# A hybrid attention and Fourier block: the Fourier input projection on sums and differences of mirrored tokens and weight columns, woven into the gate and z products, with y held in DRAM

## The chip, the cores and the metric

The kernel runs on one core of a Trainium2 chip. The metric is the time of one execution on the device in microseconds (us). Three runs of the kernel before took 2622.81 to 2623.37 us, with a median of 2623.29.

## The reference

One layer over 256 tokens of 4096 channels. After an RMS norm one wide projection gives q, k, v, the gating paths z of both branches, the Fourier input u and the gates. Attention and a two-dimensional Fourier transform work side by side; each is gated by silu(z), projected, weighted with a sigmoid gate, summed, projected again and added to x.

```python
h = rms_norm(x, norm_gain[layer])
proj = h @ w_in[layer]                       # 4096 -> 22528 columns
q, k, v, z_attn, u_four, z_four, gates = jnp.split(proj, offsets, axis=-1)
...                                          # 24 heads of 128, three dilations, softmax over all keys
branch_attn = (o_attn * jax.nn.silu(z_attn)) @ w_branch_attn[layer]

u = u_four.reshape(b, s, FOURIER_GROUPS, FOURIER_GROUP_DIM)       # 8 groups of 256 channels
y_four = jnp.fft.fft2(u, axes=(1, 3), norm="ortho").real.reshape(b, s, FOURIER_WIDTH)
branch_four = (y_four * jax.nn.silu(z_four)) @ w_branch_fourier[layer]

g_attn, g_four = jnp.split(gates + gate_bias[layer], N_BRANCHES, axis=-1)
mixed = jax.nn.sigmoid(g_attn) * branch_attn + jax.nn.sigmoid(g_four) * branch_four
x = x + mixed @ w_out[layer]
return rms_norm(x, final_norm_gain)
```

## The kernel before

Everything large is a product of an activation with 512 columns of a weight matrix. `gemm` (line 202) makes one: both token tiles (two of 128 tokens: the even and the odd ones) times 512 columns, in fp32r with three passes, since activation and weight are each split into a high and a low part: `wh` with `h_hi`, `wl` with `h_hi`, `wh` with `h_lo`. Such a product over 4096 channels has 16 steps of two slices of 128 channels, and a step has 2 x 2 x 3 = 12 matmuls of 512 columns. A 1 MB tile `wt` (four slices, 512 columns, fp32) is loaded by SyncE's queue (SP) for every second step. For each step ACT copies two slices of it to `wh` and VectorE (DVE) subtracts that from `wt` and writes `wl` (`split`, line 143). `wt`, `wh` and `wl` have three buffers each; `turn` (line 197) hands them out by turns.

The order of the products is: 2 for z of the attention (ZA), 9 for q, k, v of half the heads, 4 gates, 9 for the other half, 4 gates, the first z of the Fourier branch (ZF), then U and ZF by turns with 5 gates among them, 3 last gates; then the branches (eight pairs over 8 and 16 slices) and eight products with `w_out`. U is the Fourier input: 4 products. Each fills an accumulator pair, `u_of` copies it (with the norm's factor), `over_tokens` and `over_channels` transform it with short fp32 matmuls over the constant `dft_t` and with additions on VectorE, multiply with silu(z), transpose in 32x32 blocks and split into `y_hi` and `y_lo`, the left operand of the Fourier branch.

All that is not a product is a task: a generator that yields, before each stage, its time on VectorE and how many steps it must wait. `step` (line 126) runs once per step of a product and lets tasks go on as far as a credit allows, `BUDGET` per step. `finish` (line 119) runs tasks to their end at once. Every engine keeps the order in which the program writes its instructions (`InOrder`), so a task's stage lies in each engine's queue where `step` or `finish` put it, and an instruction that waits holds all that stands behind it on its engine. That holds for DMAs on SP too. The queue of loads runs ahead of the work only as far as the three `wt` buffers let it.

```python
def load(k):
    ...
    if k % WG == 0:
        wt = turn("wt", [P, WG, CW], F32)
        ...
            sp.dma_start(wt[:, q:q + n, :], wv[:, k + q:k + q + n, :])
    wh = turn("wh", [P, WS, CW], F32R)
    wl = turn("wl", [P, WS, CW], F32R)
    split(wt[:, k % WG:k % WG + WS, :], wh, wl)
```

The heads of the attention (`attend`) are tasks as well: scores on TensorE, mask and maximum on VectorE, the exponential on ACT, sixteen 32-row transposes on VectorE, then the product with v.

Of the kernel before, what the change touches and what calls it, by code (L numbers as in the profile page):

```python
# [17 lines left out]
P = 128  # L18
# [13 lines left out]
FW = SEQ // 4 + 1  # L32
# [3 lines left out]
GA = 4  # L36
GF = (), (8,), (9,), (10, 11, 12)
BUDGET = 1.35
CAP = 1.5
# [6 lines left out]
class InOrder:  # L46
    """An engine whose instructions keep the order that they are written in."""
# [9 lines left out]
class Clock:  # L57
    now = 0
    credit = 0.0


class Task:
# [15 lines left out]
def hybrid_block(ctx: ExitStack, tc: tile.TileContext, x, norm_gain, w_in, gate_bias, w_attn,  # L78
# [20 lines left out]
    # the function table, while the first loads are under way  # L99
# [3 lines left out]
    gates_d = dram.tile([NT, P, 2 * D], F32, name="gates_d")  # L103

# [1 line left out]
    # A task is a generator that yields, before each of its stages, the stage's time on VectorE in  # L106
    # us and the least number of steps since the stage before.
# [11 lines left out]
    def finish(these):  # L119
        while any(t in tasks for t in these):  # L120
            for t in list(these):
                finish(t.after)
                if t in tasks and not t.run(clock.now):
                    tasks.remove(t)

    def step():
        clock.now += 1
        clock.credit = min(clock.credit + BUDGET, CAP)
# [128 lines left out]
    def use(task):  # L257
        """The task that reads the product just made."""
        users[turns["acc"] % 2] = [spawn(task)]
        return users[turns["acc"] % 2]  # L260

# [1 line left out]
    h_hi = lhs.tile([P, KT, SEQ], F32R, tag="l_hi", name="h_hi")  # L263
    h_lo = lhs.tile([P, KT, SEQ], F32R, tag="l_lo", name="h_lo")
    szp = ctx.enter_context(tc.tile_pool(name="szp", bufs=1))
    sz = szp.tile([P, NT, 2 * CW], F32, tag="sz", name="sz")
# [49 lines left out]
    def norms():  # L316
        for i in range(NX):
            yield BUDGET, 0
# [8 lines left out]
    def silu(dst, ps, r):  # L327
        """dst = z * sigmoid(z), z = ps * r"""
# [4 lines left out]

    def silu_za(c, accs):
        if c == 0:
            yield from norms()
        for t in range(NT):
            yield from silu(sz[:, t, c * CW:(c + 1) * CW], accs[t], rstd[t])

    def gates(tiles, chunks):  # L340
        def gate(c, accs):
            bias, _ = tiles()
            nc.gpsimd.dma_start(bias, gate_bias[0:1, c * CW:(c + 1) * CW].to_broadcast([P, CW]))
            for t in range(NT):
                _, sg = tiles()
                yield 0.75, 0
                dve.scalar_tensor_tensor(sg, accs[t], rstd[t], bias, op0=ALU.mult, op1=ALU.add)
                yield 0.0, 1
                act.activation(sg, sg, AF.Sigmoid)
                nc.gpsimd.dma_start(gates_d[t, :, c * CW:(c + 1) * CW], sg)  # L350

        for c in chunks:
            accs = new_accs()
            gemm(accs, h_hi, h_lo, w_in, G0 + c * CW)
            use(gate(c, accs))

# [1 line left out]
    for c in range(2):  # L358
        accs = new_accs()
        gemm(accs, h_hi, h_lo, w_in, ZA0 + c * CW, **(dict(during=x_ahead, loading=x_loads) if c == 0 else {}))  # L360
        use(silu_za(c, accs))
    xs.close()

# [1 line left out]
    with ExitStack() as st:  # L365
        gp = pool(st, "gp", bufs=2)
        ap = pool(st, "ap")
        at = pool(st, "at", bufs=2)
        qp = pool(st, "qp", bufs=9)
# [60 lines left out]
        def gate_tiles():  # L430
            return gp.tile([P, CW], F32, name="bias"), gp.tile([P, CW], F32, name="sg")

        for half in range(2):
            got, made = {}, []
            for g in range(NG):
                for name, c0, fill, shape in (("q", Q0, rotated, [P, HC, SEQ]), ("k", K0, rotated, [P, HC, SEQ]),
                                              ("v", V0, values, [P, NT, CW])):
                    accs = new_accs()
                    gemm(accs, h_hi, h_lo, w_in, c0 + g * 1024 + half * CW)
                    got[name, g] = qp.tile(shape, F32, tag="qkv", name=name)  # L440
# [18 lines left out]
    with ExitStack() as st:  # L459
        fp = pool(st, "fp")  # L460
        ft = pool(st, "ft", bufs=2)
# [9 lines left out]
        flat = spawn(attn_transposed(), False)  # L471
        dft_t = fp.tile([P, NT, 2 * FW], F32, name="dft_t")
        nc.gpsimd.dma_start(dft_t, dft.rearrange("t p k -> p t k"))
        H = SEQ // 4

        def zf_of(accs, zf):
            for t in range(NT):
                yield from silu(zf[:, t, :], accs[t], rstd[t])

        def u_of(accs, u):  # L480
            # u's even and odd channels of each group, side by side
            for t in range(NT):
# [4 lines left out]
        def over_tokens(u, ab, d, ps):
            # cosine and sine sums over the tokens, from those over the even and the odd ones
            yield 0.0, 1
            pt = ps.tile([P, CW], F32, name="pt" if ps is ps_t else "sc")  # L490
            for t in range(NT):
                pe.matmul(pt[:, 2 * FW * t:2 * FW * (t + 1)], u[:, t, d, :], dft_t[:, t, :], start=True, stop=True)
            yield 0.0, LEAD
            eo = ft.tile([P, 2, 2, FW], F32, name="eo")
            act.activation(eo.rearrange("p t s k -> p (t s k)"), pt[:, :4 * FW], AF.Copy)

            def part(t, s, back):
                k = eo[:, t, s, H:0:-1] if back else eo[:, t, s, 0:H]
                return k.rearrange("p (m q) -> p m q", q=2)

            def place(s, i):
                o = ab[:, d, s, :].rearrange("p (q m) -> p m q", q=2)
                return o[:, i * H // 2:(i + 1) * H // 2, :]

            yield 1.1, 1
            for s in range(2):
                dve.tensor_add(place(s, 0), part(0, s, False), part(1, s, False))
                dve.tensor_sub(place(s, 2), part(0, s, False), part(1, s, False))
                dve.tensor_sub(place(s, 1), part(s, s, True), part(1 - s, s, True))
            dve.tensor_add(place(0, 3), part(0, 0, True), part(1, 0, True))  # L510
            dve.scalar_tensor_tensor(place(1, 3), part(0, 1, True), -1.0, part(1, 1, True),
                                     op0=ALU.mult, op1=ALU.subtract)

        def over_channels(zf, ab, c, gi, t, ps):
            yield 0.0, 1
            pt = ps.tile([P, CW], F32, name="pt" if ps is ps_t else "sc")
            for q in range(2):
                for s in range(2):
                    k = (q * 2 + s) * FW
                    pe.matmul(pt[:, k:k + FW], ab[:, gi * 2 + q, s, t * P:(t + 1) * P],  # L520
                              dft_t[:, q, s * FW:(s + 1) * FW], start=True, stop=True)
            yield 0.0, LEAD
            eo = ft.tile([P, 2, 2, FW], F32, name="eo")
            act.activation(eo.rearrange("p t s k -> p (t s k)"), pt[:, :4 * FW], AF.Copy)
            yield 1.3, 1
            lo = ft.tile([P, 2, FW], F32, name="lo")
            dve.tensor_add(lo, eo[:, 0], eo[:, 1])
            hi = ft.tile([P, 2, FW], F32, name="hi")
            dve.tensor_sub(hi, eo[:, 0], eo[:, 1])
            y = ft.tile([P, SEQ], F32, name="y")  # L530
            dve.tensor_sub(y[:, 0:H], lo[:, 0, 0:H], lo[:, 1, 0:H])
            dve.tensor_add(y[:, 2 * H - 1:H - 1:-1], hi[:, 0, 1:FW], hi[:, 1, 1:FW])
# [204 lines left out]
```

## Time and profile before

| | us |
|---|---|
| median of three runs | 2623.29 |
| span of the profiled execution | 2621.5 |
| TensorE (PE) busy | 2599.3 (99%) |
| VectorE (DVE) busy | 1724.1 (66%) |
| ACT busy | 1119.6 (43%) |
| GpSimd (POOL) busy | 41.1 (2%) |
| moved by DMA | 525.09 MB, 200 GB/s on average |

The profiled execution's own time is its span, 2621.5 us, which lies 1.8 us below the median of the runs. PE matmuls overlap in the pipeline, so a matmul's cost is read from the distance between starts and not from its length. A plain fp32 matmul (the short ones on `dft_t`, `q`, `pT`) leaves two records, an fp32r one leaves one. SPq and POOLq are the queues on which SyncE and GpSimd issue DMAs. All helpers have one line in the profile (L54), so groups are told apart by the names of their tiles.

### The profile page before, as it was taken

The page shows a single profiled execution, that of the slowest core. Times are in us where ns is not written, and L with a number is a line of the kernel's source. Part 1 is how long each engine was busy: PE and PEld are TensorE (multiplying, and loading weights), DVE is VectorE, ACT ScalarE, POOL GpSimd, SP SyncE. Part 2 cuts the span into 40 slices and gives each one's busy share as a digit, 9 for nine tenths or more (in the row PEclk, how much of TensorE's full clock was granted, in tenths as well). Part 3 has the DMA queues.
Part 4 walks back from the last instruction along what each step waited for, and adds up shares of the span by engine and source line. Part 5 has one row for each costly group of instructions (what it writes and reads, how often), then busy time and mean ns, then how long its engine had stood idle before and what let it go on. Part 6 is the DMA issues. An engine that isn't in the chain of part 4 may idle for free.

```text
span 2621.5 us, 29991 instructions
## 1 busy us (share of the span) xinstructions
PE 2599.3 (99%) x11617; PEld 2147.9 (82%) x11617; DVE 1724.1 (66%) x2847; ACT 1119.6 (43%) x1220; POOL 41.1 (2%) x74
## 2 busy tenths in 40 slices
PE   8999999999999999999999999999999999999998
PEld 7888888888888888888888888888888777888886
DVE  5566666776675757667587675757445888845554
ACT  5534343445434343444444444444444333444443
POOL 0000000000000000000000000000000000000000
PEclk9999999999999999999999999999999999999999
DMA  7655555556655555565655655556766666666674
GB/s 251 214 194 195 194 193 193 188 194 201 192 194 195 195 194 195 181 195 195 198 188 190 205 177 188 194 178 211 242 213 201 212 215 215 212 198 217 213 248 147
DMA packets 257936, 525.09 MB, mean 200 GB/s; under 512 B 9232, under 2 KB 9504, under 8 KB 257792
## 3 DMA queue, kind: packets, MB, share of 16 engines
q1 hardware_dynamic: 251344, 501.25, 58.3%
q0 software_dynamic: 6448, 21.91, 2.6%
q8 instruction: 91, 1.49, 0.2%
q14 instruction: 53, 0.43, 0.0%
HBM read 510.54 MB, written 12.58 MB: 200 GB/s over the span
## 4 chain that ended last, share of the span: by engine, by line
PE 99%; DVE 0%; DMA 0%; ACT 0%; SPq 0%; issue 0%; DVEq 0%; ACTq 0%
PE acc L54 97%; PE pt L54 1%; PE sc L54 1%; DVE wl L54 0%; DMA xt<-in_x_dram 0%; ACT u L54 0%; SPq L54 0%; DVE res L54 0%; ACT junk L54 0%; DVEq L733 0%; DVE nt L54 0%; ACT std L54 0%; DVE r L54 0%; DVE ssq L54 0%; DVE rstd_o L54 0%
## 5 line engine op out<-in xcount | busy, mean ns | idle before, releaser
L54 DVE TENSOR_TENSOR wl<-wt,wh 128x1024 fp32r<-128x1024 f32 x928 | 1134.9, 1225 | 823.0 <-ACT wh L54 817.5
L54 ACT ACTIVATE wh<-wt 128x1024 fp32r<-128x1024 f32 x928 | 980.4, 1059 | 1356.9 <-PE acc L54 1266.9
L54 PE MATMUL acc<-wh,h_hi 128*128 128x512 f32 x2816 | 1102.1, 391 | 0.0
L54 PE MATMUL acc<-wh,h_lo 128*128 128x512 f32 x2816 | 1096.9, 390 | 0.0
L54 PE MATMUL acc<-wl,h_hi 128*128 128x512 f32 x2816 | 1096.4, 389 | 0.0
L54 PEld LDWEIGHTS acc<-wh,h_lo 128*128 128x128 f32 x2816 | 528.9, 188 | 110.5
L54 PEld LDWEIGHTS acc<-wl,h_hi 128*128 128x128 f32 x2816 | 529.4, 188 | 108.3
L54 PEld LDWEIGHTS acc<-wh,h_hi 128*128 128x128 f32 x2816 | 529.3, 188 | 107.7
L54 PE MATMUL acc<-wl,m_hi 128*128 128x512 f32 x512 | 199.6, 390 | 0.0
L54 PE MATMUL acc<-wh,m_hi 128*128 128x512 f32 x512 | 199.6, 390 | 0.0
L54 PE MATMUL acc<-wh,m_lo 128*128 128x512 f32 x512 | 199.6, 390 | 0.0
L54 PEld LDWEIGHTS acc<-wh,m_lo 128*128 128x128 f32 x512 | 96.1, 188 | 20.7
L54 PEld LDWEIGHTS acc<-wh,m_hi 128*128 128x128 f32 x512 | 96.1, 188 | 20.6
L54 PEld LDWEIGHTS acc<-wl,m_hi 128*128 128x128 f32 x512 | 96.1, 188 | 20.3
L54 PE MATMUL acc<-wl,y_hi 128*128 128x512 f32 x256 | 101.1, 395 | 0.0
L54 PE MATMUL acc<-wh,y_lo 128*128 128x512 f32 x256 | 101.1, 395 | 0.0
L54 PE MATMUL acc<-wh,y_hi 128*128 128x512 f32 x256 | 101.0, 395 | 0.0
L54 DVE STREAM_TRANSPOSE mT<-m 32x128 f32<-32x128 f32 x256 | 77.4, 302 | 3.8
L54 DVE STREAM_TRANSPOSE pT<-pe 32x128 f32<-32x128 f32 x256 | 77.2, 302 | 4.0
L54 DVE STREAM_TRANSPOSE yT<-y 32x64 f32<-32x64 f32 x256 | 60.3, 236 | 3.6
L54 DVE STREAM_TRANSPOSE q<-m 32x128 f32<-32x128 f32 x192 | 58.0, 302 | 3.1
L54 DVE STREAM_TRANSPOSE k<-m 32x128 f32<-32x128 f32 x192 | 58.0, 302 | 3.1
(104 smaller groups left out, 1003.1 us busy)
## 6 DMA issues: line engine op xcount, KB each, us to landing
wt<-in_w_in_dram SPq DMA_DIRECT2D x351, 1024.0 KB, 5.1
wt<-in_w_out_dram SPq DMA_DIRECT2D x64, 1024.0 KB, 5.5
wt<-in_w_branch_fourier_dram SPq DMA_DIRECT2D x32, 1024.0 KB, 5.5
wt<-in_w_branch_attn_dram SPq DMA_DIRECT2D x16, 1024.0 KB, 5.5
ga<-gates_d POOLq DMA_DIRECT2D x16, 512.0 KB, 7.0
xt<-in_x_dram SPq DMA_DIRECT2D x16, 256.0 KB, 7.4
gates_d<-sg POOLq DMA_DIRECT2D x16, 256.0 KB, 2.7
gates_d<-z POOLq DMA_DIRECT2D x16, 256.0 KB, 3.8
```

The source lines that it names most:

```text
L54: return lambda *a, **k: self.tc.keep_in_program_order(f(*a, **k))
```

## The change

**The Fourier input.** The transform over 256 tokens and 256 channels has mirror symmetry: cosine sums need only x[s] + x[256-s], sine sums only x[s] - x[256-s], along both axes. The change makes these sums and differences before the product. `fold` makes them of the tokens of h (with the norm's factor from `norm_rows`): 128 folded rows of sums and 128 of differences, split into `f_hi` and `f_lo`; token 128 stands apart (`h128`). `u_sums` makes them of the weight's columns, in place in the raw tile `wu` (sums, 2 x 129 = 258 columns for two groups) and in `wo` (differences, 2 x 127 = 254), and gathers token 128's part on VectorE (`ea`). `u_split` splits them with ACT and VectorE; `u_multiply` multiplies: sums with sums and differences with differences, 2 slices x 2 x 3 = 12 matmuls of 258 or 254 columns. The 4 U products of 768 matmuls of 512 columns go.

**Where it stands.** These 64 u steps (two halves of the channels, four blocks of 512 columns, eight pairs of slices) lie between the steps of 12 products, nine gates and the four ZF: `u_hook` runs at each step of them, one u step every three steps, its three parts by turns.

```diff
+    def u_load(n):
...
+            raws[n] = U["fp"].tile([P, 2, CW], F32, name=f"wu{n % 2}")
...
+            sp.dma_start(raws[n], w_in[k * P:(k + 2) * P, c0:c0 + CW].rearrange("(k p) n -> p k n", p=P))
...
+        for j in range(2):
+            dve.tensor_tensor(o[:, j], near[:, j], far[:, j], op=ALU.subtract)
+            dve.tensor_tensor(near[:, j], near[:, j], far[:, j], op=ALU.add)
...
+                dve.scalar_tensor_tensor(a, e, row, a, op0=ALU.mult, op1=ALU.add)
...
+    def u_split(n):
+        w, o = raws.pop(n).rearrange("p k (g i) -> p k g i", g=2), parts[n]
+        uh, ul = (turn(v, [P, WS, CW], F32R) for v in ("wh", "wl"))
+        for src, s in ((w[:, :, :, 0:FW], slice(0, 2 * FW)), (o, slice(2 * FW, CW))):
+            for j in range(2):
+                h, l = (a[:, j, s].rearrange("p (g i) -> p g i", g=2) for a in (uh, ul))
+                act.activation(h, src[:, j], AF.Copy)
+                dve.tensor_tensor(l, src[:, j], h.bitcast(F32), op=ALU.subtract)
...
+                pe.matmul(out_, a, uh[:, j, s], start=(k == 0), stop=False)
+                pe.matmul(out_, a, ul[:, j, s], start=False, stop=False)
+                pe.matmul(out_, b, uh[:, j, s], start=False, stop=(k == HK - 1))
...
+        n, i = h // 3, h % 3
+        if i == 0:
+            if 0 < n <= len(usteps):
+                u_multiply(n - 1)
+            if n < len(usteps):
+                u_sums(n)
+        elif n < len(usteps):
+            if i == 1:
+                u_split(n)
+            else:
+                u_load(n + 2)
...
+    gates(1, at=(8, x_done))
+    u_load(0)
+    u_load(1)
+    clock.budget = BUDGET_U
+    for kind in "ggggggzgzzgz":
```

`wu` has two buffers. In the stretch `wh` and `wl` have a fourth buffer (`spare_u`). The budget of other tasks there is 0.9 instead of 1.35.

**The transform.** `mix` is a task per block of 512 columns. For each of two groups it has five fp32 matmuls of 130 columns (over tokens), eight ACT copies that put cosine and sine parts in order, four fp32 matmuls of 256 columns (over channels) and one multiplication with silu(z). The result y is written to `y_d` in DRAM. The tasks `over_tokens` and `over_channels` with their butterflies go.

```diff
+            y = U["ft"].tile([P, NT, SEQ], F32, name="y")
+            dve.tensor_tensor(y, ys.rearrange("p (t n) -> p t n", t=NT), zfs[c][:, :, g * SEQ:(g + 1) * SEQ], op=ALU.mult)
+            n0 = c * CW + g * SEQ
+            nc.gpsimd.dma_start(y_d[:, :, n0:n0 + SEQ].rearrange("t p n -> p t n"), y)
```

**The order of the products.** Gate 0 (during which x is transposed, as ZA was), gate 1 (norms, then `folding`), the stretch of 12, the two ZA, then the attention with one gate behind half 0 and three behind half 1 (`GA`), two gates during which y is read back (`yb`), transposed on TensorE and split (`y_transposed`), then branches and output as before. The heads of half 0 may run on into half 1 and are finished at its fourth product; q, k and v have 12 buffers instead of 9. `finish` now runs each task to its end before the next.

```diff
-        while any(t in tasks for t in these):
-            for t in list(these):
-                finish(t.after)
-                if t in tasks and not t.run(clock.now):
+        for t in list(these):
+            finish(t.after)
+            while t in tasks:
+                if not t.run(clock.now):
                     tasks.remove(t)
...
+                    if len(got) == 3:
+                        finish(heads)
...
+            gates(GA[half])
+        finish(heads)
```

**The order on SP.** Before, in any product: each load waits for the DMA semaphore that it reuses (DMAHW) and for VectorE (DVE), which frees its buffer. Behind `wt` stands the buffer's number.

```order
L54 DMA wt2_1127<-in_w_in_dram 128x4x512 [waits DMAHW5_49,DVE_49]
L54 DMA wt0_1178<-in_w_in_dram 128x4x512 [waits DMAHW6_49,DVE_49]
L54 DMA wt1_1203<-in_w_in_dram 128x4x512 [waits DMAHW7_49,DVE_49]
L54 DMA wt2_1243<-in_w_in_dram 128x4x512 [waits DMAHW0_49,DVE_49]
L54 DMA wt0_1282<-in_w_in_dram 128x4x512 [waits DMAHW1_49,DVE_49]
```

In the stretch of the changed kernel, `wu0` and `wu1` are the raw weights of the u steps:

```order
L55 DMA wt2_2034<-in_w_in_dram 128x4x512 [waits DMAHW5_49]
L55 DMA wu0_2066<-in_w_in_dram 128x2x512 [waits DMAHW6_49,DVE_49]
L55 DMA wt0_2080<-in_w_in_dram 128x4x512 [waits DMAHW7_49]
L55 DMA wt1_2143<-in_w_in_dram 128x4x512 [waits DMAHW0_49]
L55 DMA wu1_2149<-in_w_in_dram 128x2x512 [waits DMAHW1_49,DVE_49]
L55 DMA wt2_2198<-in_w_in_dram 128x4x512 [waits DMAHW2_49]
L55 DMA wu0_2230<-in_w_in_dram 128x2x512 [waits DMAHW3_49,DVE_49]
L55 DMA wt0_2244<-in_w_in_dram 128x4x512 [waits DMAHW4_49]
L55 DMA wu1_2307<-in_w_in_dram 128x2x512 [waits DMAHW6_49,DVE_49]
```

The wait for VectorE moved from every `wt` to the `wu` loads, and the `wt` loads stand behind these in the queue.

**The order on VectorE at the same place.** Before, in a product of the attention: the two `wl` of each `wt`, two steps to a tile.

```order
L54 TENSOR_TENSOR wl2_2011<-wt1_2008,wh2_2010 128x1024 [waits DMAHW7_49,Activation_49]
L54 TENSOR_TENSOR wl0_2027<-wt1_2008,wh0_2026 128x1024 [waits Activation_49]
L54 TENSOR_TENSOR wl1_2045<-wt2_2042,wh1_2044 128x1024 [waits DMAHW0_49,Activation_49]
L54 TENSOR_TENSOR wl2_2061<-wt2_2042,wh2_2060 128x1024 [waits Activation_49]
L54 TENSOR_TENSOR wl0_2096<-wt0_2093,wh0_2095 128x1024 [waits DMAHW1_49,Activation_49]
```

In the stretch, a u step's sums (`wo`, `wu1`, `ea0`) stand before the second `wl` of `wt0`, its splits (`wl3` from `wu1`, then from `wo`) behind it, and the next `wt1` after these:

```order
L55 TENSOR_TENSOR wl0_1555<-wt2_1526,wh0_1554 128x1024 [waits Activation_49]
L55 TENSOR_TENSOR wl1_1575<-wt0_1572,wh1_1574 128x1024 [waits DMAHW5_49,Activation_49]
L55 TENSOR_TENSOR wo_1590<-wu1_1461 128x254 [waits DMAHW2_49,DVE_49]
L55 TENSOR_TENSOR wu1_1461<-wu1_1461 128x2x127 [waits DVE_49]
L55 TENSOR_TENSOR wo_1590<-wu1_1461 128x254
L55 TENSOR_TENSOR wu1_1461<-wu1_1461 128x2x127 [waits DVE_49]
L55 SCALAR_TENSOR_TENSOR ea0_774<-wu1_1461,h128_772,ea0_774 128x258
L55 SCALAR_TENSOR_TENSOR ea0_774<-wu1_1461,h128_772,ea0_774 128x258 [waits DVE_49]
L55 TENSOR_TENSOR wl2_1610<-wt0_1572,wh2_1609 128x1024 [waits Activation_49]
L55 TENSOR_TENSOR wl3_1614<-wu1_1461,wh3_1613 128x258 [waits Activation_49] x2
L55 TENSOR_TENSOR wl3_1614<-wo_1590,wh3_1613 128x254 [waits Activation_49] x2
L55 TENSOR_TENSOR wl0_1638<-wt1_1635,wh0_1637 128x1024 [waits DMAHW6_49,Activation_49]
```

The `wu1` here is the buffer that a later `wu1` load on SP overwrites; its last readers on VectorE are the two `wl3` from `wu1`.

**The order on VectorE at the end of the attention.** Before, where the last head ends (`pT` its transposes, `sz` its result), with gate and ZF products running on:

```order
L54 TENSOR_TENSOR wl2_9223<-wt1_9220,wh2_9222 128x1024 [waits DMAHW0_49,Activation_49]
L54 STREAM_TRANSPOSE pT_9182<-pe_9144 32x4x32 x4
L54 TENSOR_TENSOR wl0_9243<-wt1_9220,wh0_9242 128x1024 [waits Activation_49]
L54 STREAM_TRANSPOSE pT_9182<-pe_9144 32x4x32 x4
L54 TENSOR_TENSOR wl1_9289<-wt2_9286,wh1_9288 128x1024 [waits DMAHW1_49,Activation_49]
L54 TENSOR_TENSOR wl2_9293<-wt2_9286,wh2_9292 128x1024 [waits Activation_49]
L54 SCALAR_TENSOR_TENSOR sg_9283<-acc10_8925,rstd_x_130,bias_9279 128x512 [waits DMASW7_49,DMASW5_49,PE_49]
L54 TENSOR_TENSOR wl0_9312<-wt0_9309,wh0_9311 128x1024 [waits DMAHW2_49,Activation_49]
L54 SCALAR_TENSOR_TENSOR sg_9318<-acc11_8926,rstd_x_130,bias_9279 128x512 [waits DMASW0_49,PE_49]
L54 TENSOR_TENSOR wl1_9333<-wt0_9309,wh1_9332 128x1024 [waits DVE_49,Activation_49]
L54 SCALAR_TENSOR_TENSOR sz_92<-pt_9262,rden_9180,sz_92 128x128
L54 TENSOR_TENSOR wl2_9354<-wt1_9351,wh2_9353 128x1024 [waits DMAHW3_49,DVE_49,Activation_49]
```

In the changed kernel, from the maximum of the last head but one to the first `wl` of the next product:

```order
L55 TENSOR_REDUCE mx_14366<-sm_14364 128x1 [waits DVE_49]
L55 TENSOR_SCALAR nm_14368<-mx_14366 128x1 [waits DVE_49]
L55 RECIPROCAL rden_14373<-den_14370 128x1 [waits Activation_49]
L55 STREAM_TRANSPOSE pT_14375<-pe_14371 32x4x32 x16
L55 SCALAR_TENSOR_TENSOR sz_6913<-pt_14392,rden_14373,sz_6913 128x128 [waits DVE_49,PE_49]
L55 TENSOR_TENSOR sm_14402<-sc_14398,mask_t_7203 128x512 [waits PE_49]
L55 TENSOR_REDUCE mx_14404<-sm_14402 128x1 [waits DVE_49]
L55 TENSOR_SCALAR nm_14406<-mx_14404 128x1 [waits DVE_49]
L55 RECIPROCAL rden_14411<-den_14408 128x1 [waits Activation_49]
L55 STREAM_TRANSPOSE pT_14413<-pe_14409 32x4x32 x16
L55 SCALAR_TENSOR_TENSOR sz_6913<-pt_14430,rden_14411,sz_6913 128x128 [waits DVE_49,PE_49]
L55 TENSOR_TENSOR wl0_14457<-wt1_14454,wh0_14456 128x1024 [waits DMAHW1_49,Activation_49]
```

Between the two last heads and behind them stood `wl` of running products; now none does until the last `sz`.

More of the change, by code (lines that the diff above doesn't have):

```diff
@@ L31 @@
 SCALE = DH ** -0.5
[L32 removed]
+FW = P + 1
+UK = 16
 WG = 4
@@ new lines, in hybrid_block, with gates, folding @@
+    gated = [0]
+    def gates(n, after=(), **kw):
+        for _ in range(n):
+            c = gated[0]
+            gated[0] += 1
+            accs = new_accs()
+            gemm(accs, h_hi, h_lo, w_in, G0 + c * CW, **kw)
+            use(gate(c, accs), after)
+    fo = ctx.enter_context(ExitStack())
+    U = {}
+    HK = KT // 2
+    def folding():
+        fp = U["fp"] = pool(fo, "fp")
+        U["ft"] = pool(fo, "ft")
+        spare.append(pool(fo, "spare_u"))
+        dft_t = fp.tile([P, 906], F32, name="dft_t")
+        nc.gpsimd.dma_start(dft_t, dft)
+        U["ct"], U["st"], U["at"] = (dft_t[:, 130 * i:130 * (i + 1)] for i in range(3))
+        U["cc"], U["sc"] = dft_t[:, 390:390 + SEQ], dft_t[:, 390 + SEQ:390 + 2 * SEQ]
+        U["sgn"] = dft_t[:, 902:903]
+        U["hi"] = fp.tile([P, HK, 2, P], F32R, name="f_hi")
+        U["lo"] = fp.tile([P, HK, 2, P], F32R, name="f_lo")
+        U["h128"] = fp.tile([P, KT], F32, name="h128")
+        U["rows"] = fp.tile([P, SEQ], F32, name="rows")
+        U["ea"] = [fp.tile([P, 2, 2, FW], F32, name=f"ea{c}") for c in range(4)]
+        U["od"] = [fp.tile([P, 2, P], F32, name=f"od{c}") for c in range(4)]
+        U["z"] = fp.tile([P, 2, P], F32, name="z")
+        for a in [U["z"], *U["od"]]:
+            nc.gpsimd.memset(a, 0.0)
+        U["norm"] = spawn(norm_rows(), False)
+        U["fold"] = [U["norm"]]
+        for b in range(HK // 4):
+            U["fold"].append(spawn(fold(b), False, U["fold"][-1:]))
@@ new lines, in norm_rows @@
+    def norm_rows():
+        ones = U["ft"].tile([P, P], F32, name="ones")
+        nc.gpsimd.memset(ones, 1.0)
+        dg = U["ft"].tile([P, NT, P], F32, name="dg")
+        yield 0.0, 0
+        for t in range(NT):
+            act.activation(dg[:, t, :], ident, AF.Copy, scale=rstd[t])
+        yield 0.0, 1
+        sc = ps_s.tile([P, CW], F32, name="sc")
+        for t in range(NT):
+            pe.matmul(sc[:, t * P:(t + 1) * P], ones, dg[:, t, :], start=True, stop=True)
+        yield 0.0, 1
+        act.activation(U["rows"], sc[:, :SEQ], AF.Copy)
@@ new lines, in u_hook, with zf_of @@
+    def u_hook(k):
+        if k < 0:
+            return
+        h = hooks[0]
+        hooks[0] += 1
+        n, i = h // 3, h % 3
+        if i == 0:
+            if 0 < n <= len(usteps):
+                u_multiply(n - 1)
+            if n < len(usteps):
+                u_sums(n)
+        elif n < len(usteps):
+            if i == 1:
+                u_split(n)
+            else:
+                u_load(n + 2)
+    zfs, zf_made = {}, {}
+    def zf_of(c, accs):
+        zf = zfs[c] = U["ft"].tile([P, NT, CW], F32, name="zf")
+        for t in range(NT):
+            yield from silu(zf[:, t, :], accs[t], rstd[t])
@@ new lines, in hybrid_block, with x_done @@
+    accs = new_accs()
+    gated[0] = 1
+    gemm(accs, h_hi, h_lo, w_in, G0, during=x_ahead, loading=x_loads)
+    normed = spawn(norms())
+    use(gate(0, accs), [normed])
+    def x_done():
+        finish([normed])
+        xs.close()
+        folding()
+    gates(1, at=(8, x_done))
[3 more added lines that the diff above has]
+    for kind in "ggggggzgzzgz":
+        if kind == "g":
+            gates(1, during=u_hook)
+        else:
+            c = len(zf_made)
+            accs = new_accs()
+            gemm(accs, h_hi, h_lo, w_in, ZF0 + c * CW, during=u_hook)
+            finish(mixing)
+            zf_made[c] = use(zf_of(c, accs))
@@ L334, in silu_za, with mixed @@
+    clock.budget = BUDGET
     def silu_za(c, accs):
-        if c == 0:
-            yield from norms()
         for t in range(NT):
             yield from silu(sz[:, t, c * CW:(c + 1) * CW], accs[t], rstd[t])
[L340 to L355, printed above, removed]
+    def mixed():
+        finish(mixing)
+        spare.clear()
+        fo.close()
@@ L487, in over_tokens @@
[L487 to L532, printed above, removed]
-            dve.tensor_sub(y[:, 2 * H:3 * H], hi[:, 0, 0:H], hi[:, 1, 0:H])
-            dve.tensor_add(y[:, 4 * H - 1:3 * H - 1:-1], lo[:, 0, 1:FW], lo[:, 1, 1:FW])
-            dve.tensor_mul(y, y, zf[:, t, gi * SEQ:(gi + 1) * SEQ])
-            yT = ft.tile([P, 2, P], F32, name="yT")
-            yield from flipped(yT, blocks(y))
-            b = c * 4 + gi * 2
-            yield from splitting(yT, y_hi[:, b:b + 2, t * P:(t + 1) * P], y_lo[:, b:b + 2, t * P:(t + 1) * P])
```

218 lines of the change are left out of this document (140 added, 78 removed).

## The prediction

> **What bounds the kernel now.** I read the page's busy line first, then the chain that ended last, the idle time of the costliest groups, the waits, and last a stretch of the timeline.
>
> ```profile
> span 2621.5 us, 29991 instructions
> PE 2599.3 (99%) x11617; PEld 2147.9 (82%) x11617; DVE 1724.1 (66%) x2847; ACT 1119.6 (43%) x1220; POOL 41.1 (2%) x74
> PE 99%; DVE 0%; DMA 0%; ACT 0%; SPq 0%; issue 0%; DVEq 0%; ACTq 0%
> ```
>
> TensorE is busy for 99% of the span and makes up 99% of the chain: nothing else ends last anywhere but at the edges. Its timeline shows what one product costs:
>
> ```profile
> 899.64 0.39 PE L54 MATMUL acc<-wh,h_hi 128*128 128x512 f32 x1
> 899.87 0.39 PE L54 MATMUL acc<-wl,h_hi 128*128 128x512 f32 x1
> 900.09 0.39 PE L54 MATMUL acc<-wh,h_lo 128*128 128x512 f32 x1
> 900.32 0.39 PE L54 MATMUL acc<-wh,h_hi 128*128 128x512 f32 x1
> ```
>
> Three starts take 0.68 us, so a 512-column matmul is worth 0.2267 us whatever its recorded length. A step of 12 takes 2.72, a product of 16 steps 43.5. The engines that feed it have slack, and where that slack lies is the point of this forecast:
>
> ```profile
> L54 DVE TENSOR_TENSOR wl<-wt,wh 128x1024 fp32r<-128x1024 f32 x928 | 1134.9, 1225 | 823.0 <-ACT wh L54 817.5
> L54 ACT ACTIVATE wh<-wt 128x1024 fp32r<-128x1024 f32 x928 | 980.4, 1059 | 1356.9 <-PE acc L54 1266.9
> SPq L54 <- DVE wl L54: 2198.2, 431, 12.0
> 579.88 18.62 SPq L54 DMA_DIRECT2D wt<-in_w_in_dram  x4
> wt<-in_w_in_dram SPq DMA_DIRECT2D x2, 1024.0 KB, 5.0
> 10.00:20.00 10.00, 9.93 (x39) 8.15 (x40) 6.17 (x9) 5.57 (x9) 0.00 (x0) 1.00 1.05 392
> ```
>
> ACT waits for TensorE to free a `wh`; VectorE waits for ACT; SyncE's queue waits for VectorE to free a `wt`, and issues at once when it does. Four 1 MB issues lie in 18.62 us, one per 5.44. A transfer lands 5.0 us after its issue (DMA view from 579.85 to 585.3 us), but it was issued two to three buffers (11 to 16 us) ahead of its use. So 5 us of latency is hidden by lead alone. The last row (a window of the start, where DMA is full) gives 392 GB/s as the rate when transfers queue up.
>
> **What the change removes.** Four U products: 768 x 0.2267 = 174.1 us. The old Fourier matmuls:
>
> ```profile
> L54 PE MATMUL sc<-dft_t,ab 128*128 128x65 f32 x64 | 8.5, 275 | 0.0
> L54 PE MATMUL pt<-dft_t,u 128*128 128x130 f32 x32 | 6.0, 294 | 0.9 <-ACT u L54 0.6
> 682.48 1.06 PE L54 MATMUL pt<-v,pT 128*128 128x128 f32 x8
> 683.29 0.48 PE L54 MATMUL acc<-wh,h_hi 128*128 128x512 f32 x1
> ```
>
> Short fp32 matmuls come as two records each. In the third row eight records take up 0.81 us to the next start, about 0.11 with the edges (0.112 from start to start); I take 0.112 for each record up to 130 columns. The 192 records of the old transform go (two groups of 64 over `ab`, two of 32 over `u`): 21.5 us, and 0.9 of idle time with them. What is left of the span is 2621.5 - 174.1 - 21.5 - 0.9 = 2425.0. VectorE's old butterflies and `yT` transposes lay beside TensorE and give nothing.
>
> **What it adds to TensorE in the stretch.** 64 u steps of 12 matmuls with 258 or 254 columns, between the steps of 12 products (522.3 us by themselves). No row has such a matmul: the nearest are the 112 ns record from below and 227 ns of a 512-column one from above. I take 0.12, close to half of 227, so 92.2 us, and TensorE alone would need 614.5. The ends are 86 and 174 us.
>
> **What it does to the queue of weights.** This is the term that decides. `u_load(n+2)` overwrites the raw weights of u step n, so this DMA waits for VectorE's second operation of `u_split(n)`, the last that reads them. On SyncE it stands among the `wt` loads, and those behind it wait too, though their own buffers are free already: in the order they have no VectorE wait left. The lead of two to three buffers is lost; every second or third step a `wt` starts only when VectorE has come to a point near the work that this `wt` is for.
>
> ```profile
> L54 DVE TENSOR_TENSOR y<-y,zf 128x256 f32<-128x256 f32 x16 | 6.8, 426 | 0.5
> L54 DVE SCALAR_TENSOR_TENSOR m<-acc,rstd_x,rope_t 128x256 f32<-128x256 f32 x48 | 20.8, 475 | 0.0
> 902.29 1.23 DVE L54 TENSOR_TENSOR wl<-wt,wh 128x1024 fp32r<-128x1024 f32 x1 [1.49 <-ACT wh L54]
> 903.44 1.52 DVE L54 SCALAR_TENSOR_TENSOR m<-acc,rstd_x,rope_t 128x512 f32<-128x512 f32 x3
> ```
>
> Back to back, the next start lies 1.15 behind a `wl`, 0.08 less than its length. Over two u periods (six steps, three `wt`, two `wu`) the loop closes like this:
> - `wu` is issued, then `wt` behind it: the `wt` lands after 5.0 + 0.52 MB at 392 GB/s (1.3) = 6.3 us; `wh` 1.06; `wl` 1.15; the six operations of `u_sums` (four at 0.43, two at 0.475, less three overlaps of 0.08) 2.4; the second `wl` of that `wt` 1.15; two operations of `u_split` 0.8. Sum 12.9.
> - next period, in which the `wt` behind the `wu` is used after the sums: 6.3 + 1.06 + 1.15 + 0.8 = 9.3.
>
> Together 22.2 us for six steps, where TensorE has 6 x 2.72 + 24 x 0.12 = 19.2. Thirty-two such pairs take 710. Other VectorE work in the stretch is 55 us by the same rows (folds, gate and silu products, additions, y); the order puts about a fifth of it between a landing and the next release: 11. So the **stretch takes about 720 us**, 197.7 more than its products. With VectorE's short operations a sixth shorter or longer, the same loop gives 703 or 744. Since TensorE then waits, 0.12 for its new matmuls does not matter: up to 0.245 they hide in the loop.
>
> The Trainium skill, "DMA: Bandwidth & Descriptors", section "Anatomy of one DMA — SWDGE (gpsimd) path", fits about 2.0 us plus the bytes at 436 GB/s (for another kind of queue). By that 1 MB would take 4.4 us, where this trace has 5.0 and so disagrees, and the pair would land after 5.6 us, which would make the loop 20.8 and the stretch 677.
>
> **What it adds elsewhere.** Head rows that the tail rests on:
>
> ```profile
> L54 DVE STREAM_TRANSPOSE pT<-pe 32x128 f32<-32x128 f32 x256 | 77.2, 302 | 4.0
> L54 DVE TENSOR_TENSOR sm<-sc,mask_t 128x512 f32<-128x512 f32 x16 | 10.9, 682 | 0.0
> L54 DVE TENSOR_REDUCE mx<-sm 128x1 f32<-128x512 f32 x16 | 11.0, 686 | 0.6
> L54 ACT ACTIVATE pe<-sm,nm 128x512 f32<-128x512 f32 x16 | 11.6, 723 | 0.7
> L54 ACT ACTIVATION_READ_ACCUMULATOR pe<-sm,nm 128x1 f32 x16 | 3.0, 187 | 0.0
> L54 DVE TENSOR_SCALAR nm<-mx 128x1 f32<-128x1 f32 x16 | 2.5, 153 | 0.6
> L54 DVE RECIPROCAL rden<-den 128x1 f32<-128x1 f32 x16 | 2.5, 156 | 0.0
> L54 DVE SCALAR_TENSOR_TENSOR sz<-pt,rden,sz 128x128 f32<-128x128 f32 x16 | 5.5, 346 | 2.7 <-PE pt L54 2.7
> L54 ACT ACTIVATE junk<-xt 128x512 f32<-128x512 f32 x16 | 10.0, 623 | 0.3
> L54 PE MATMUL sc<-k,q 128*128 128x256 f32 x32 | 9.6, 379 | 0.0
> L54 DVE TENSOR_TENSOR y_lo<-yT,y_hi 128x256 fp32r<-128x256 f32 x16 | 6.6, 418 | 0.0
> L54 ACT ACTIVATE y_hi<-yT 128x256 fp32r<-128x256 f32 x16 | 6.6, 410 | 13.7 <-DVE yT L54 13.7
> ga<-gates_d POOLq DMA_DIRECT2D x16, 512.0 KB, 7.0
> ```
>
> - **End of the attention, 15.** Only three gate products follow half 1, and its last two heads are run to their end one after the other behind the last product's matmuls. Each is a chain: mask 0.68, maximum 0.69, its scaling 0.15, exp 0.72 and the read of its sum 0.19, reciprocal 0.16, sixteen transposes of 0.302 (4.8), eight records of 0.112 (0.9), the final product 0.35: 8.6. Two make 17.3, and the next product's first `wl` (1.2) is queued behind them on VectorE; TensorE still has about 3.5 us of products when they begin. Before, the heads ended inside products.
> - **End of half 0, 2.** The heads left over at the fourth product of half 1 are finished there; mostly between products.
> - **Slow clock behind these idle times, 2.5.** In the start's rows a 512-column matmul takes 0.427 instead of 0.227 for the first 4 us:
>
> ```profile
> 11.63 0.63 PE L54 MATMUL acc<-wh,h_lo 128*128 128x512 f32 x1
> 12.05 0.63 PE L54 MATMUL acc<-wh,h_hi 128*128 128x512 f32 x1
> ```
>
> The Trainium skill, "TensorE: Matmul & The Clock Gate", "Part 1: The HAM clock gate", says that the clock halves when the engine has idled and comes back after about 3.4 us; the trace's start agrees (4 us), an idle stretch in mid-run it cannot show. Without this the sum is 2.5 less.
> - **Mixing, 5.7.** Eight rounds of five fp32 matmuls of 130 columns (10 x 0.112) and four of 256 (8 x 0.217, between 0.112 and twice 0.227): 2.86 each. Six fall where TensorE waits in the stretch and are free, two come after it. Were that cover gone, 17.2 more.
> - **Norms on ACT in the second product, 2.9.** Junk squares of 0.62 + 0.19 stand four and six at a time between the `wh`, where two did; one `wl` comes 2.9 late.
> - **y again, 7.8.** 32 transposes through TensorE at 0.11, as for the other records of 128 columns: 3.5. The way through DRAM costs nothing: POOL's queue carries eight more writes and four more reads, the nearest read takes 7.0 us, and the whole attention lies between; only the first read, issued as the gates begin, has four steps (10.9) to cover it. The last four groups are forced at the end of the gates (0.43 on TensorE, 0.41 to 0.62 on ACT, 0.42 to 0.69 on VectorE, two buffers), then `wh` and `wl` of the next product: 4.3.
> - Last u step 1.4, row norms 0.5.
>
> Sum 37.8; a loss of half of it or a half more is possible (19 to 57).
>
> **The sum.** 2425.0 + 197.7 + 37.8 = 2660.5 as a span. The median of the runs before, 2623.29, is 1.8 above the span, so the time is **2662 us**, 1.5% slower. Without the blocked queue the arithmetic saving would stand.
>
> **The rivals.**
> - *The queue does not bind (faster).* If `wu` is released early enough, or transfers land faster than read here, TensorE stays the bound: 2425.0 + 92.2 + 37.8 + 17.2 of mixing that is no longer hidden = 2572.2, with 1.8 it is 2574. For it: 99% today, and 19.2 against 22.2 is no wide margin. Against it: SyncE waits on VectorE 431 times, longest 12.0 us, so that a wait put into its order is felt by all that stand behind. It decides at a loop of 21.3 us for two periods with the other VectorE work in it (681 us in all): below that the change gains.
> - *The pair lands sooner.* If the data of `wu` move while the `wt` behind it is still in its issue and set-up, only half of the 1.3 us is added, and the pair lands 5.6 us after the `wu`: a loop of 20.8 and a stretch of 677. The time is then 2425.0 + 154.7 + 37.8 + 1.8 = 2619, within 0.2%. Single transfers of 5.0 cannot tell; the fit of the Trainium skill above would have it so.
> - *Transfers share the rate (slower still).* Of the three `wt` in two periods one is issued right behind another. Where two lie together in the start, they took 7.4:
>
> ```profile
> wt<-in_w_in_dram SPq DMA_DIRECT2D x7, 1024.0 KB, 7.4
> ```
>
> One landing in two periods 0.7 to 1.4 later gives 743 to 765: 2684 to 2707.
> - *The narrow matmuls are not narrow in time.* At 0.227 TensorE needs 696.6, still less than 720: no change; at 0.27 it would be 730, 2672. If it were true together with a queue that does not bind, 2425.0 + 174.3 + 55 + 1.8 = 2656, so the saving depends on half width being half time.
>
> **Chances and range.** Forecast, the loop as worked out (2640 to 2684): 0.52. Sharing: 0.22. Larger tails on top of either, above 2707: 0.05. The queue does not bind: 0.13, around 2574, tails making it 2560 to 2590. Between them, 2590 to 2618: 0.03. Within 0.2%, which is 5.2 us and about what a measurement of this kernel can tell from no change: 0.05. Faster is 0.16, same 0.05, slower 0.79. The range for 8 in 10 runs from 2572 to 2708; the likeliest case alone has 2640 to 2684.
>
> **What would show it.** Right: in the profile after, SyncE's queue waits in the stretch for `wl` of the u parts, ACT's `wh` waits for `wt`'s DMA, TensorE's share falls in slices of the first third, and two u periods take 22 us against 19.2. The end of the attention shows one TensorE gap of 15 to 20 us with matmuls of 0.43 behind it. Wrong: `wh` still waits for TensorE throughout the stretch (the first rival), or 256-column matmuls start 0.2 apart or more. The forecast fails if a `wt` lands much below 6 us behind its `wu`, or if VectorE comes to `u_split` earlier relative to the `wt` than its order suggests.

## The result, and the profile after

| | before | after |
|---|---|---|
| median, us | 2623.33 (4 runs) | 2712.53 (2712.14 to 2713.43, 4 runs) |
| profiled span, us | 2621.5 | 2711.7 |

The ratio is 1.034, with a 95% interval of 1.0326 to 1.0355: the change makes the kernel 3.4% slower. The forecast of 2662 had the sign and, as the next sections show, the mechanism that blocks the queue, but it was 50 us short, and the time lies above its range.

The page of the changed kernel, its busy line and its chain:

```profile
span 2711.7 us, 30469 instructions
PE 2587.0 (95%) x11605; PEld 2118.4 (78%) x11605; DVE 1820.6 (67%) x2991; ACT 1125.8 (42%) x1471; POOL 50.9 (2%) x92
PE 70%; DMA 11%; DVE 9%; issue 3%; ACT 2%; SPq 0%; ACTq 0%; DVEq 0%
PE acc L55 68%; DMA wt<-in_w_in_dram 11%; DVE wl L55 5%; ACT wh L55 2%; PE pt L55 1%; DVE wu L55 1%; PE sc L55 1%; DVE ea L55 1%; DVE wo L55 1%; DVE pT L55 0%; DVE e L55 0%; DVE f L55 0%; DVE sg L55 0%; SPq L55 0%; DVE f_lo L55 0%
```

TensorE has less to do than its 2599.3 us before, yet it makes up 70% of the chain instead of 99%. The rest of the chain is a ring: a weight load, ACT's and VectorE's split of it, VectorE's work on the u weights. The waits say the same (total us, times, longest):

```profile
ACT wh L55 <- DMA wt<-in_w_in_dram: 314.8, 57, 9.0
ACT wh L55 <- DVE wu L55: 48.0, 58, 3.7
SPq L55 <- DVE wl L55: 2396.6, 391, 28.3
```

The first of these was not among the long waits before. Where the time went is seen by windows: the stretch of 12 products with the u steps, from its first matmul to the first matmul of the product after it, and the three gate products' last one at the end of the attention. Columns are the window, its length, busy time of PE, PEld, DVE, ACT and POOL, granted clock, DMA share and GB/s.

```profile
113.00:879.30 766.30, 687.45 (x3182) 555.31 (x3181) 514.79 (x910) 311.80 (x564) 18.96 (x33) 0.96 0.54 187
1910.80:1976.30 65.50, 52.62 (x244) 44.23 (x242) 44.57 (x100) 25.73 (x30) 1.62 (x3) 0.93 0.44 140
```

The stretch takes 766.3 us; the forecast had 720, and by its terms TensorE alone would need 632 with the mixing. So 46 of the 50 us that the forecast is short lie in this one window.

One turn of the ring in VectorE's and SyncE's timelines (start, length, instruction):

```profile
382.45 0.37 SPq L55 DMA_DIRECT2D wu<-in_w_in_dram  x1
382.86 0.47 SPq L55 DMA_DIRECT2D wt<-in_w_in_dram  x1
...
395.63 0.37 SPq L55 DMA_DIRECT2D wu<-in_w_in_dram  x1
```

```profile
390.06 1.23 DVE L55 TENSOR_TENSOR wl<-wt,wh 128x1024 fp32r<-128x1024 f32 x1 [5.84 <-ACT wh L55]
391.20 0.42 DVE L55 TENSOR_TENSOR wo<-wu 128x254 f32<-128x254 f32 x1
391.65 0.42 DVE L55 TENSOR_TENSOR wu<-wu 128x254 f32<-128x254 f32 x1
392.00 0.42 DVE L55 TENSOR_TENSOR wo<-wu 128x254 f32<-128x254 f32 x1
392.45 0.42 DVE L55 TENSOR_TENSOR wu<-wu 128x254 f32<-128x254 f32 x1
392.79 1.01 DVE L55 SCALAR_TENSOR_TENSOR ea<-wu,h,ea 128x258 f32<-128x258 f32 x2
393.71 1.22 DVE L55 TENSOR_TENSOR wl<-wt,wh 128x1024 fp32r<-128x1024 f32 x1
394.85 0.76 DVE L55 TENSOR_TENSOR wl<-wu,wh 128x258 fp32r<-128x258 f32 x2
```

From `wu`'s issue at 382.45 the `wt` behind it lands at 388.87 (6.42), ACT's `wh` starts at 388.97, VectorE runs `wl`, the sums, `wl` and the two splits until 395.61, and SyncE issues the next `wu` at 395.63: 13.18 us, where the forecast's list had 12.9. The short turn, from 395.63 to the next `wu` at 405.19, takes 9.56 (forecast 9.3). Two such turns, undisturbed, take 22.7; over the 61 turns from 115 to 856 us two turns take 24.3 on average.

What makes the mean longer is, for the most part, the landing. A pair here is a `wu` and the `wt` behind it, its landing the time from `wu`'s issue to the landing of that `wt`. The pairs are sorted by whose packets the DMA queues carried besides in that time:

```
other traffic beside the pair          pairs   mean   least  most (us)
none                                    34     6.41   6.24   6.59
GpSimd's (bias, gates_d, y_d)           10     7.73   6.53   9.07
a fetch of instructions                 17     7.23   6.22   8.26
both                                     1    10.34  10.34  10.34
```

Two examples from the DMA view of the pair's window, first one with a fetch (issued at 274.60, landing 7.65), then one with GpSimd's traffic (at 831.91, 7.98): queue, packets, MB, share; then the issues with the us to landing of each by itself (`wt` is issued 0.42 after `wu`, to be added for the pair).

```profile
q1 hardware_dynamic: 800, 1.57, 62.4%
q8 instruction: 1, 0.02, 1.1%
...
wt<-in_w_in_dram SPq DMA_DIRECT2D x1, 1024.0 KB, 7.2
wu<-in_w_in_dram SPq DMA_DIRECT2D x1, 512.0 KB, 4.0
```

```profile
q1 hardware_dynamic: 800, 1.57, 53.7%
q0 software_dynamic: 155, 0.50, 21.0%
...
wt<-in_w_in_dram SPq DMA_DIRECT2D x1, 1024.0 KB, 7.6
wu<-in_w_in_dram SPq DMA_DIRECT2D x1, 512.0 KB, 5.2
```

Before, TensorE lost next to nothing to loads: a weight tile came two to three buffers ahead. In the ring a delay is passed on in full: what follows a landing, up to the next `wu`, is as long behind a late one as behind a quick one. It is 3.13 us in the short turn after a landing of 6.28 (issue at 351.97) and of 8.05 (250.20), and 6.76 in the long one after 6.37 (843.02) and 8.02 (796.06).

### The profile page after: what moved, and what is told of

Read it like the earlier page. It is cut to its first block, busy times and chain, and to the rows that moved or that the text cites. A ratio compares the mean times of both kernels' runs of the same rounds, so it can differ in the third digit from the quotient of the medians.

```text
span 2711.7 us, 30469 instructions
## 1 busy us (share of the span) xinstructions
PE 2587.0 (95%) x11605; PEld 2118.4 (78%) x11605; DVE 1820.6 (67%) x2991; ACT 1125.8 (42%) x1471; POOL 50.9 (2%) x92
## 4 chain that ended last, share of the span: by engine, by line
PE 70%; DMA 11%; DVE 9%; issue 3%; ACT 2%; SPq 0%; ACTq 0%; DVEq 0%
PE acc L55 68%; DMA wt<-in_w_in_dram 11%; DVE wl L55 5%; ACT wh L55 2%; PE pt L55 1%; DVE wu L55 1%; PE sc L55 1%; DVE ea L55 1%; DVE wo L55 1%; DVE pT L55 0%; DVE e L55 0%; DVE f L55 0%; DVE sg L55 0%; SPq L55 0%; DVE f_lo L55 0%
## 5 line engine op out<-in xcount | busy, mean ns | idle before, releaser
L55 DVE TENSOR_TENSOR wl<-wt,wh 128x1024 fp32r<-128x1024 f32 x864 | 1052.8, 1224 | 781.1 <-ACT wh L55 777.8
L55 ACT ACTIVATE wh<-wt 128x1024 fp32r<-128x1024 f32 x864 | 906.0, 1057 | 1315.0 <-PE acc L55 939.8
L55 PE MATMUL acc<-wh,h_hi 128*128 128x512 f32 x2560 | 1020.0, 398 | 40.4 <-ACT wh L55 40.4
L55 PE MATMUL acc<-wl,h_hi 128*128 128x512 f32 x2560 | 1016.1, 397 | 42.0 <-DVE wl L55 42.0
L55 PE MATMUL acc<-wh,h_lo 128*128 128x512 f32 x2560 | 1009.8, 394 | 0.0
L55 PEld LDWEIGHTS acc<-wl,h_hi 128*128 128x128 f32 x2560 | 487.8, 191 | 162.8 <-DVE wl L55 65.2
L55 PEld LDWEIGHTS acc<-wh,h_hi 128*128 128x128 f32 x2560 | 487.4, 190 | 151.3 <-ACT wh L55 53.0
L55 PE MATMUL pt<-wl,f_hi 128*128 128x258 f32 (+1 forms) x256 | 73.0, 285 | 0.0
L55 ACT ACTIVATE wh<-wu 128x258 fp32r<-128x258 f32 x128 | 49.8, 413 | 55.6 <-DVE wu L55 45.1
L55 PE MATMUL pt<-wh,f_hi 128*128 128x258 f32 (+1 forms) x256 | 72.6, 283 | 0.0
```

The source lines that it names most:

```text
L55: return lambda *a, **k: self.tc.keep_in_program_order(f(*a, **k))
```

## The experiments

The first four ask whether the ring is the cause (against VectorE and ACT being simply too busy, or TensorE's clock), and test two terms of the sum by themselves. Each was timed beside the kernel before on the same chip (2623.89 there, 2623.69 for the second group); the changed kernel's 2712.53 us is that of the result above.

**e1_load_later.** Nothing but the place of the raw u load in the program is moved.

```diff
-                u_load(n + 2)
+                u_load(n + 1)
...
     u_load(0)
-    u_load(1)
```

> Only the place of the raw u weights' load on SyncE's queue moves: u step n+1 is loaded at the last third of u step n, three steps later than in the changed kernel, with the same two buffers, so that its wait for VectorE is met sooner. Theory 1 (the wait of this load blocks the weight loads behind it): the stretch becomes bound by TensorE, 522 + 92 + 17 = 632 to 650 us instead of 766, the whole 2575 to 2600 us; ACT's waits for the wt DMA fall from 315 us to under 60. Rival 2 (VectorE and ACT cannot keep up with the added splits and sums, whatever SyncE does): 2690 to 2713. Rival 3 (TensorE's slow clock in the stretch is a cause by itself): about 25 us of slow matmuls stay, 2610 or more.

Measured: 2590.63 us (2588.54 to 2592.98), ratio to before 0.9874 (0.9859 to 0.9888). With the same instructions on TensorE, VectorE and ACT, the same buffers and the same bytes, 122 us are gone. The stretch, and the wait of ACT for the loads:

```profile
113.20:756.60 643.40, 637.94 (x3181) 540.00 (x3181) 517.16 (x911) 320.29 (x564) 18.96 (x33) 1.00 0.67 221
ACT wh L55 <- PE acc L55: 1056.6, 630, 5.1
ACT wh L55 <- DMA wt<-in_w_in_dram: 1.9, 2, 1.6
```

643.4 us instead of 766.3, TensorE busy for 638 of them at full clock; ACT waits for TensorE again, and its 314.8 us of waiting for `wt` are 1.9. VectorE is as busy as in the changed kernel (517 against 515), so rival 2 falls. Rival 3 falls too: the granted clock is 1.00, so the slow clock went with TensorE's idle time.

**e6_wu_pool.** The other way to free SyncE's queue.

```diff
-            sp.dma_start(raws[n], w_in[k * P:(k + 2) * P, c0:c0 + CW].rearrange("(k p) n -> p k n", p=P))
+            nc.gpsimd.dma_start(raws[n], w_in[k * P:(k + 2) * P, c0:c0 + CW].rearrange("(k p) n -> p k n", p=P))
```

> The raw u weights are loaded from GpSimd's queue instead of SyncE's, at the same places of the program. Theory 1: no weight load stands behind such a wait any more, stretch 632 to 660, the whole 2575 to 2610. Rival 2: 2690 or more. A side effect that either theory allows: the gates' bias loads then stand behind these waits on GpSimd's queue and may hold VectorE by some us each.

Measured: 2590.47 us (2588.11 to 2592.51), ratio 0.9872 (0.9858 to 0.9887), the same as e1 within the spread. Here the wait for VectorE is still one step behind its release, and GpSimd's queue spends 468.1 us in 56 such waits, but no weight load stands behind it. So it is not the wait that costs, it is what is queued behind it. The side effect on the gates did not show: the stretch takes 643.4 us as in e1.

**e3_no_gate_dma.** Does traffic beside the pair lengthen the ring? The gates of the stretch (eight; its 12 products are eight gates and the four ZF, not nine gates as said ahead of the prediction) go without their bias, and zeros are stored for them later, so this kernel does not give the layer's result.

```diff
+        mute = 2 <= c < 10
+        if mute:
+            nc.gpsimd.memset(bias, 0.0)
+        else:
+            nc.gpsimd.dma_start(bias, gate_bias[0:1, c * CW:(c + 1) * CW].to_broadcast([P, CW]))
...
+            if not mute:
+                nc.gpsimd.dma_start(gates_d[t, :, c * CW:(c + 1) * CW], sg)
...
+        for c in range(2, 10):
+            for t in range(NT):
+                nc.gpsimd.dma_start(gates_d[t, :, c * CW:(c + 1) * CW], zt)
```

> The eight gates of the stretch load no bias (a zero tile instead) and store nothing; zeros are stored for them during the attention. Theory 1 with the landing as the term that was too small: nine of the pairs of a raw load and a weight load landed 0.9 to 3.9 us late beside these transfers, 16 us in sum, and the stretch falls by 12 to 20 us: 2692 to 2701. If other traffic does not lengthen the loop: 2708 to 2714.

Measured: 2706.02 us (2698.53 to 2709.41), 6.5 less than the changed kernel in a spread of 11. Both expectations miss: less than 12 to 20, and not nothing. In its profile the stretch takes 761.0 us instead of 766.3. That alone shows little: e4 below changes nothing in the stretch, and its profile has 761.5 there. The pairs say more. Six of them still lie beside GpSimd's packets (11 before), and what the landings of these take beyond 6.45 us falls from 16.7 to 4.4 us in sum. But for the pairs beside a fetch of instructions alone the same sum rises from 13.2 to 17.0, and over all pairs it falls from 28.7 to 21.4 (e4: 25.4). So the landings beside GpSimd's packets get rarer with these packets; that the kernel gets faster by it, some 7 us at most, is not shown clear of what varies from run to run.

**e4_finish_abreast.** The end of the attention, by the loop of the kernel before.

```diff
-        for t in list(these):
-            finish(t.after)
-            while t in tasks:
-                if not t.run(clock.now):
-                    tasks.remove(t)
+        while any(t in tasks for t in these):
+            for t in list(these):
+                finish(t.after)
+                if t in tasks and not t.run(clock.now):
+                    tasks.remove(t)
```

> Only the loop that runs tasks to their end is that of the kernel before (a stage of each in turn); of the instructions only the last two heads of the attention change place. The forecast's chain of two heads, one after the other: the second head's mask, maximum, scaling, exponential, reciprocal (2.6), its product and result (1.3) lie beside the first head's transposes: 3 to 4.5 us less, 2708 to 2709.5, all of it in the third gate product behind half 1 (65.5 us now). If TensorE's gap there is from something else: no change.

Measured: 2707.85 us (2703.23 to 2710.22), 4.7 less than the changed kernel. The spread alone would not carry that; the window does. The third gate product behind half 1 takes 61.9 us instead of 65.5:

```profile
1904.80:1966.70 61.90, 51.98 (x243) 43.77 (x242) 44.57 (x100) 25.72 (x30) 1.62 (x3) 0.93 0.47 149
```

This product takes 61.9 in e5 below as well. The 3.6 us are the overlap of the two heads' chains, as the expectation had it.

The second group asks how much lead the ring needs, and whether the repairs add.

**e7_lead2.** The same load, two steps behind its release (one in the changed kernel, four in e1).

```diff
             if n < len(usteps):
+                u_load(n + 1)
                 u_sums(n)
...
-            else:
-                u_load(n + 2)
...
     u_load(0)
-    u_load(1)
```

> The raw weights of u step n+1 are loaded at the first third of u step n: on SyncE's queue two steps behind the release that they wait for, where the changed kernel has one step and e1_load_later four. Theory 1, by its loop: of the two landings that stood in a row in two u periods one now falls out, since the weight load behind it is used only after the next release; a pair is 9.4 for the period that still has it and about 9.6 of TensorE's work for the other, near TensorE's own 19.2 to 19.7. So nearly all comes back at once: stretch 645 to 675, the whole 2592 to 2622. A rival in which the wait costs in proportion to the lead lost (a third of the way from 2712 to 2591 by one step of three) has 2655 to 2685.

Measured: 2597.1 us (2595.79 to 2597.25), ratio 0.9899 (0.9882 to 0.9915). One more step brings back 115 of the 122 us, as the loop said and a loss in proportion did not. The stretch takes 649.6 us (from 112.4 to 762.0), and ACT's waits for `wt` there are between those of the two neighbours:

```profile
ACT wh L55 <- DMA wt<-in_w_in_dram: 74.8, 25, 8.1
```

By the loop's sum there is a threshold: while a turn is shorter than TensorE's work of the same steps, its parts cost nothing; above that, each microsecond of a part is paid. e7 and the changed kernel lie on its two sides; no kernel close to it was run.

**e5_later_abreast and e8_budget.** e1 with e4's loop, and then with more credit for the heads in the last three gate products.

```diff
+            if half == 1:
+                clock.budget = 1.5
             gates(GA[half])
         finish(heads)
+        clock.budget = BUDGET
```

> e1_load_later with the loop that runs tasks to their end as before. The two effects lie in different stretches and add: 2590.6 less 3.5 to 4.5, 2586 to 2587. If they share a cause, 2590.

> e5_later_abreast with the tasks' budget at 1.5 instead of 1.35 in the three gate products behind half 1. Forecast's reading of the end of the attention (too few products for the heads): 48 steps let 7 us more of the heads' VectorE work run inside products, 4 to 8 us less at the end: 2578 to 2583. If VectorE in these products is already the bound, the products get longer and nothing is won: 2586 to 2590.

Measured: 2586.23 us (2585.15 to 2587.02), ratio 0.9857 (0.9842 to 0.9872), and 2584.16 us (2583.11 to 2584.78), ratio 0.9849 (0.9834 to 0.9864). The first is as expected, the effects add. The second gains 2.1 where 4 to 8 were expected:

```profile
1786.40:1846.40 60.00, 51.61 (x244) 43.40 (x242) 43.16 (x97) 24.90 (x28) 1.62 (x3) 0.93 0.46 154
```

The product at the end is 1.9 shorter (60.0 against 61.9), and the two gates before it are as long as they were. But the product behind it takes 47.8 us instead of 46.2, and the two profiles (2585.2 and 2581.3 us) differ by as much, 3.9 us, already where the stretch begins, ahead of the edit. So it is not shown that the 2.1 us come from the credit. Most of it did not become extra work inside the gates; why not I did not follow up. Each head's stages also wait a set number of steps for each other. e8_budget is the fastest version found, 1.5% faster than the kernel before.

## Why the prediction was wrong

**Right.** The sign. That TensorE would stop being the bound in the stretch alone, and why: the wait of `wu` on SyncE with the `wt` loads behind it. e1, e6 and e7 show it from three sides. The arithmetic under it: the narrow matmul, forecast at 0.12, takes 0.12 (twelve of them from 510.78 to 512.22):

```profile
510.78 0.28 PE L55 MATMUL pt<-wh,f_hi 128*128 128x258 f32 x1
...
512.11 0.28 PE L55 MATMUL pt<-wh,f_lo 128*128 128x254 f32 x1
512.22 0.39 PE L55 MATMUL acc<-wh,h_hi 128*128 128x512 f32 x1
```

The two turns of the loop, undisturbed, came out near the forecast too (13.2 and 9.6 against 12.9 and 9.3).

**Right in kind, not in size.** Without the blocked queue the kernel is faster than before, as the first rival said. It gave 2574; e1, with the attention's tail as it was, has 2590.6. Of these 17 us 12 lie in the stretch (643.4 against 614.5 + 17.2 = 631.7). By the distances between starts in e1 the u matmuls take 92.4 us there (forecast 92.2) and the mixing 15.4 (17.2), but the products' own matmuls 535.6 instead of 522.3. Some 7 of these 13 us are nine short waits of TensorE, and most of the rest is 2 ns more for each of the matmuls.

**Wrong: the term "the `wt` lands after 5.0 + 0.52 MB at 392 GB/s (1.3) = 6.3 us".** It was read from a quiet stretch of the trace and put into the sum as a constant, for all 62 landings of the ring. Undisturbed it is 6.41, and the mean is 6.9: 62 x 0.6 = 38 of the 46 us that the stretch is longer. About 7 of the 38 are the quiet value itself (6.41 for 6.3), 17 lie in the pairs beside GpSimd's packets, 14 in those beside a fetch of instructions alone. The other 8 are a balance: the rest of the turns is 13 us longer than the forecast had it, 6 of them the 0.1 us from each landing to the start of `wh`, and what lies outside the 61 turns is 5 us shorter.

The forecast listed GpSimd's queue only to say that y's way over it costs nothing. That is said of its own way, not of the loads beside it in a loop that has no slack; fetches of instructions it does not mention. The trace before could have warned: of the four loads in the forecast's row from 579.88, two of which gave its 5.0, the last was issued at 598.14 beside a store on GpSimd's queue and landed after 6.7 us. The mean and not the quiet value belongs into such a loop.

One bound of the loop's sum is off as well, though nothing else rests on it: with VectorE's short operations a sixth shorter its own terms give about 697 us and not 703.

The time lies above **the range** for the same reason. It had the landing longer only by a rival with another mechanism: that a `wt` with a second `wt` right behind it shares the rate with it. That rival's 743 to 765 us come close by chance. The trace speaks against it: of the 34 pairs without other traffic, the 19 with a second `wt` right behind them land after 6.44 us on average, the 15 without one after 6.38. That is 0.06 apart, where the rival had 0.7 to 1.4.

**The faster landing** of 5.6 us per pair, an estimate by the fit that the Trainium skill's page "DMA: Bandwidth & Descriptors" (section "Anatomy of one DMA — SWDGE (gpsimd) path") gives for another kind of queue, occurs in no pair. The least is 6.22.

**The tails** came out at 41.5 against 37.8 us, by the lengths of the products in both traces. After the stretch 6.2 (forecast 5.7 + 1.4), norms 4.1 (3.4), half 0 1.6 (2). The end of half 1 has 15.4 (15), with two gaps of TensorE where the forecast had one of 15 to 20, one for each head:

```profile
1963.30 2.07 PE L55 MATMUL pt<-v,pT 128*128 128x128 f32 x8 [5.20 <-DVE pT L55]
1965.16 1.69 PE L55 MATMUL sc<-k,q 128*128 128x256 f32 x6
1974.54 2.08 PE L55 MATMUL pt<-v,pT 128*128 128x128 f32 x8 [7.68 <-DVE pT L55]
```

The eight short records take 2 us there instead of 0.81: the clock is already slow between the two heads. The two gates with y and the start of the branches have 14.2 (y 7.8 and the clock 2.5 in the forecast). Two things were not in the sum at all: the removed Fourier work was worth 24.7 us of longer products before, not 22.4, and the first product starts at 13.9 us instead of 10.6, behind 5.03 us in which TensorE waits for VectorE's first `h_lo`. All kernels with the change show this start (13.1 to 14.5); its cause was not looked for.

## What to carry to other kernels

A DMA that must wait for a buffer takes away the lead of every load behind it on its queue; put it where its buffer has been free for longer than a landing, or on a queue with nothing urgent behind it. Before adding a load to a queue that runs ahead, close the loop on paper (release, landing, each engine's part until the next release) and compare one turn with the bound engine's work in the same steps. If it closes near or above that, every part counts, and with its mean, other traffic included, not with the value from a quiet place.

## What the runs showed of the hardware that was not expected

TensorE's clock can fall after quite short idle times in the middle of a run. In the changed kernel's stretch:

```profile
148.02 0.39 PE L55 MATMUL acc<-wh,h_lo 128*128 128x512 f32 x1
151.19 0.80 PE L55 MATMUL acc<-wh,h_hi 128*128 128x512 f32 x1 [2.78 <-ACT wh L55]
152.44 0.80 PE L55 MATMUL acc<-wl,h_hi 128*128 128x512 f32 x1 [0.46 <-DVE wl L55]
153.04 0.63 PE L55 MATMUL acc<-wh,h_lo 128*128 128x512 f32 x1
153.47 0.63 PE L55 MATMUL acc<-wh,h_hi 128*128 128x512 f32 x1
```

After gaps of 2.78 and 0.46 us the starts lie 0.43 apart instead of 0.227; from 150.6 to 157.4 us the granted clock is 0.50. Shorter gaps did it too: 1.32 and 0.76 us (before 269.05 and 270.31). The length alone does not decide, for after 1.82 and 0.76 us (before 202.10 and 203.36) the clock stayed full. Over the whole stretch the granted clock is 0.96. What this costs there was not tried; TensorE mostly waits anyway.

A fetch of instructions, one packet of 16 KB or 8 KB, often goes with a megabyte-sized load that lands over a microsecond later. All pairs above 6.8 us without GpSimd's packets have such a fetch in their window, up to 8.26 against 6.41. What matters seems to be when it starts. In the traces of the changed kernel, e3 and e4 together, and beside no packets of GpSimd's, a packet of the queue `q8 instruction` that starts within 5.3 us of `wu`'s issue lies in 26 pairs, and 24 of them land after more than 6.8 us; a later one lies in 16 pairs, and 2 of them do. This is a coincidence in time that the traces show, not tried by an experiment.
